# Hybrid decoder block on one core: how many attention turns go with each dense output of the input projection

## The chip, the core and the metric

The kernel runs on one core of a Trainium2 chip. The metric is device time in microseconds of one launch, the median of several runs; a profiled execution of the same program gives the trace. The engines are PE (TensorE, matrix products), DVE (VectorE), ACT (ScalarE), POOL (GpSimd) and SP, which issues most DMAs. Each engine works through its own queue in program order, and waits at an instruction until what that one needs has been signalled by the others.

## The reference

x has 2048 rows of 1024 values.

```python
hn = rmsnorm(h, norm1_g)
proj = hn @ w_in                       # 512 pool columns, then 512 each of q, k, v
y_pool = pool_mixer(u_pool)            # 4 groups of 128, causal means over 2, 4, 8, 16 rows, less the row; then a 128x128 map
o = stick_breaking_attention(q, k, v)  # 8 heads of 64: A[t,s] = sigmoid(z_ts) * prod_(s<j<t) (1 - sigmoid(z_tj))
mixed = concat(rmsnorm(y_pool), rmsnorm(o))
h = h + mixed @ w_out
h = h + relu(rmsnorm(h) @ w_up) ** 2 @ w_down
y = rmsnorm(h)
```

## The kernel before

The rows are cut into four tiles of 512 (tiles 0 to 3). Everything lies transposed: 128 channels on the partitions, 512 rows of a tile along the free axis. Every fp32 product is made of three reduced-precision ones, from a high and a low part of either side; a split (line 145 on ACT for the high part, 146 on DVE for the low) makes these.

The **front** is the first third of the program. It computes the input projection, 16 *dense outputs* per tile: four pool groups (numbers 0 to 3, with windows 2, 4, 8, 16), and q, k and v of four pairs of heads (4 to 15). A dense output is 8 x 3 matmuls of 512 columns (lines 177 to 179) into one of two PSUM buffers `pd`. Its weights are split on ACT and DVE first (`hl<-raw`). Then an evacuation follows: q and k are split and stored to DRAM (`qk`), v is transposed first (`vf`, `ptv`, `vt`). A pool output goes further (`pool_group`): ACT copies it to `u`, DVE adds shifted copies (`s`, line 400; one addition for window 2, up to four for window 16), forms `pl` (line 403), splits it (`pls`, high part on ACT, low part on DVE), and PE maps it with three matmuls (`pp`, lines 410 to 412), which need `pls`.

Between the matmuls of the dense outputs lies the attention, which looks only at the near keys of each row, in 64 *turns* (8 heads x 4 tiles x 2 halves). A turn starts one unit and takes the two before it a stage further. A unit has three stages: logits on PE (`pz`, lines 630 and 631), two sigmoids on ACT (`sh`, `sg`), a mask on POOL (`sg`, line 661), a running product on DVE (`pc`, line 663) and a product (`sg`, line 672); then four transposes on PE (`pta`, line 677) and a split (`at`); then up to six small products on PE (`po`, line 689), and, after every second unit, a sum of halves (`ot`, lines 647 on ACT and 648 on DVE).

How many turns go with a dense output is set by a **ratio**. A dense output adds the ratio to a debt, half of it in its middle and half at its end, and each turn pays back 0.27:

```python
if k == n // 2 - 1:
    advance(state["ratio"] / 2)        # line 181, in products
...
while state["due"] > 0 and todo:       # in advance
    state["due"] -= next(todo[0])      # a turn yields 0.27
```

So a ratio of 0.4 means some three turns with two dense outputs, 0.15 about one with two. When no turn is open, the debt is set to zero. The order of the front is: tile 0 (q, k, v of two pairs, then pool); q, k, v of the other two pairs, for tiles 0 and 1 in turn; tile 1 (pool, then its first two pairs); tile 2 (first two pairs, then pool); the other two pairs for tiles 2 and 3; tile 3 (first two pairs, then pool). Alongside, the next tile is normed piece by piece (`nt`, `h`). What this code emits is a program order with priorities; a scheduler then places each engine's instructions, so that the final order of an engine differs from the order in which the code is written.

Behind the front come the output projection (ratio 0.6, `RATIO_TAIL`, while turns are left) and the feed-forward part, which this code does not touch.

## Time and profile before

| | us |
|---|---|
| median of three runs | 1903.73 (1903.68 to 1907.18) |
| the profiled execution | 1902.05 |
| its span, first to last instruction | 1900.3 |
| PE busy in it | 1868.9 |
| DVE busy in it | 1481.2 |

A PE busy time is the union of its matmuls' spans. A matmul of 512 columns lasts 0.39 us by itself, and the next starts 0.23 us after it where nothing is missing. The granted clock is the share of 2.4 GHz that PE is given; 0.5 is the lower level, 1.2 GHz. The bracket at the end of a timeline row is the idle time of the engine ahead of that instruction, and what ended it.

### The profile page before, as it was taken

Reading aid. Unit: us, or ns where it says so; the run is one execution under the profiler, and the core shown is the slowest. Engines: PE = TensorE matmul, PEld = TensorE weight load, DVE = VectorE, ACT = ScalarE, POOL = GpSimd, SP = SyncE. Lnnn points to the kernel's source line nnn. Section 1 sums busy time; section 2 is a strip of 40 time slices with the busy share of each in tenths; the row PEclk is TensorE's granted clock in tenths of the full one; section 3 lists DMA queues with packets and bytes.
Section 4 is the critical chain, followed back from the end, with each engine's and each line's share of the span. In section 5 each row is a group of like instructions: output and inputs, shape, how many; then the busy total and the mean of one; then the engine's idle time right before and its main releaser. Section 6 shows DMA issues by size and latency. Waiting matters only on the chain.

```text
span 1900.3 us, 26640 instructions
## 1 busy us (share of the span) xinstructions
PE 1868.9 (98%) x8883; PEld 1554.3 (82%) x8883; DVE 1481.2 (78%) x2151; ACT 1025.2 (54%) x1616; POOL 238.5 (13%) x463
## 2 busy tenths in 40 slices
PE   9999999999999999999999999999999999999997
PEld 7788788788888888777888888887888888888886
DVE  6887789678866886778799988786666677988774
ACT  6565567455644465554567555554332665656543
POOL 0233234122321050000000000000010010020120
PEclk9999999999999999999999999999999999999998
DMA  7676596699888777787899888889999899999852
GB/s 226 212 255 201 177 313 224 194 322 315 281 310 312 278 252 254 284 303 274 307 358 328 303 308 281 298 284 333 388 313 330 281 317 307 332 294 341 289 206 91
DMA packets 222164, 535.91 MB, mean 282 GB/s; under 512 B 26048, under 2 KB 32192, under 8 KB 218176
## 3 DMA queue, kind: packets, MB, share of 16 engines
q1 hardware_dynamic: 217264, 525.46, 79.4%
q0 software_dynamic: 4608, 8.39, 2.4%
q8 instruction: 72, 1.18, 0.3%
q14 instruction: 76, 0.62, 0.1%
q10 hardware_dynamic: 144, 0.26, 0.0%
HBM read 349.46 MB, written 184.55 MB: 281 GB/s over the span
## 4 chain that ended last, share of the span: by engine, by line
PE 50%; DMA 5%; DVE 2%; issue 1%; ACT 1%; POOL 0%; SPq 0%; DVEq 0%; ACTq 0%
PE pb L1291 14%; PE pY L1118 13%; PE pb L1468 12%; PE pZ L1118 7%; PE pX L1118 3%; DMA ar<-sd 1%; DMA hn<-hs 1%; DMA ar<-sdi 1%; PE pb L1408 1%; DMA td<-t 0%; DMA t<-in_w_down_dram 0%; DMA b<-in_w_down_dram 0%; DMA wr<-in_w_down_dram 0%; DVE ad L146 0%; DVE hw L146 0%
## 5 line engine op out<-in xcount | busy, mean ns | idle before, releaser
L1118 PE MATMUL pY<-sa,hw 128*128 128x512 f32 x1536 | 366.3, 390 | 1.9 <-ACT u L1041 1.9
L1118 PEld LDWEIGHTS pY<-sa,hw 128*128 128x128 f32 x1536 | 287.9, 188 | 63.0 <-ACT u L1041 3.4
L1291 PE MATMUL pb<-ad,wd 128*128 128x512 f32 x1344 | 305.4, 389 | 0.7 <-DVE ad L146 0.7
L177 PE MATMUL pd<-h,hl 128*128 128x512 f32 x752 | 297.9, 396 | 1.5 <-DVE qk L146 1.3
L178 PE MATMUL pd<-h,hl 128*128 128x512 f32 x752 | 297.0, 395 | 0.3 <-DVE h L146 0.3
L179 PE MATMUL pd<-h,hl 128*128 128x512 f32 x752 | 297.3, 395 | 0.0
L1291 PEld LDWEIGHTS pb<-ad,wd 128*128 128x128 f32 x1344 | 252.1, 188 | 53.8 <-DVE ad L146 1.5
L1468 PE MATMUL pb<-ad,wd 128*128 128x512 f32 x1104 | 253.9, 390 | 0.9 <-ACT ad L145 0.9
L1468 PEld LDWEIGHTS pb<-ad,wd 128*128 128x128 f32 x1104 | 206.5, 188 | 44.6 <-ACT ad L145 1.3
L146 DVE TENSOR_TENSOR ad<-ar,ad 128x1024 fp32r<-128x1024 f32 x160 | 194.1, 1221 | 44.1 <-ACT ad L145 43.5
L145 ACT ACTIVATE ad<-ar 128x1024 fp32r<-128x1024 f32 x160 | 168.4, 1054 | 95.7 <-PE pb L1468 31.9
L1118 PE MATMUL pZ<-sa,hw 128*128 128x512 f32 x768 | 186.8, 390 | 1.7 <-DVE a L1061 1.7
L1118 PEld LDWEIGHTS pZ<-sa,hw 128*128 128x128 f32 x768 | 143.9, 188 | 32.7 <-DVE a L1061 3.0
L145 ACT ACTIVATE hl<-raw 128x512 fp32r<-128x512 f32 x168 | 104.1, 629 | 115.6 <-PE pd L179 76.7
L177 PEld LDWEIGHTS pd<-h,hl 128*128 128x128 f32 x752 | 142.2, 189 | 29.0 <-DVE qk L146 1.8
L179 PEld LDWEIGHTS pd<-h,hl 128*128 128x128 f32 x752 | 142.0, 189 | 28.2 <-DVE hl L146 0.5
L178 PEld LDWEIGHTS pd<-h,hl 128*128 128x128 f32 x752 | 142.2, 189 | 27.1 <-DVE h L146 0.7
L146 DVE TENSOR_TENSOR hl<-raw,hl 128x512 fp32r<-128x512 f32 x168 | 115.1, 690 | 46.9 <-ACT hl L145 46.5
L1035 ACT ACTIVATE a<-a 128x512 f32<-128x512 f32 x96 | 60.1, 629 | 89.6 <-DVE a L1077 38.5
L146 DVE TENSOR_TENSOR hw<-rt,hw 128x512 fp32r<-128x512 f32 x128 | 86.5, 686 | 25.2 <-ACT hw L145 25.1
L145 ACT ACTIVATE wd<-wq 128x1024 fp32r<-128x1024 f32 x56 | 59.4, 1060 | 77.1 <-PE pb L1291 68.4
L146 DVE TENSOR_TENSOR wd<-wq,wd 128x1024 fp32r<-128x1024 f32 x56 | 68.5, 1222 | 34.3 <-ACT wd L145 32.8
(218 smaller groups left out, 2737.3 us busy)
## 6 DMA issues: line engine op xcount, KB each, us to landing
ar<-sd SPq DMA_DIRECT2D x96, 512.0 KB, 5.9
ar<-sdi SPq DMA_DIRECT2D x64, 512.0 KB, 5.6
rb<-in_w_up_dram SPq DMA_DIRECT2D x30, 1024.0 KB, 6.2
sd<-a SPq DMA_DIRECT2D x104, 256.0 KB, 5.2
raw<-in_w_in_dram SPq DMA_DIRECT2D x50, 512.0 KB, 4.6
sdi<-hr SPq DMA_DIRECT2D x96, 256.0 KB, 5.4
wr<-in_w_down_dram SPq DMA_DIRECT2D x48, 512.0 KB, 5.7
sd<-s SPq DMA_DIRECT2D x88, 256.0 KB, 4.9
```

What stands on the lines that cost most here:

```text
L145: nc.scalar.activation(hi, src, AF.Copy)
L146: return nc.vector.tensor_tensor(lo, src, hi.bitcast(F32), ALU.subtract)
L177: nc.tensor.matmul(ps, hl[:, 0, c], hi, start=(k == 0), stop=False)
L178: nc.tensor.matmul(ps, hl[:, 0, c], lo, start=False, stop=False)
L179: last_mm[0] = nc.tensor.matmul(ps, hl[:, 1, c], hi, start=False, stop=(k == n - 1))
L1035: nc.scalar.activation(t, src, AF.Relu)
L1118: nc.tensor.matmul(t, w[:, wx, c], a[:, ax, c % 2], start=first and c == 0 and x == 0, stop=last and c == G - 1 and x == 2, skip_group_che ...
L1291: nc.tensor.matmul(b, t[:, wx, 2 * (kk % 2) + c, i * P:(i + 1) * P], a[:, ax, c], start=p in ("P1", "P5", "P2") and kk == 0 and c == 0 and ...
L1408: nc.tensor.matmul(b[:, cols], block(t, wx, c, n), a[:, ax, c, cols], start=False, stop=(i == 1 and c == 1 and x == 2), skip_group_check=True)
L1468: nc.tensor.matmul(ps[q, n], block(t, wx, c, n), left_[q][:, ax, c], start=(n_ in ("P1", "P3") and kk == 0 and c == 0 and x == 0), stop=(n ...
```

## The change

The table of six ratios becomes a table by tile pair, stretch and kind of output: a pair of numbers stands for (q, k or v; pool), and the middle number is that of the stretch in which two tiles alternate. In the first pair (tiles 0 and 1) the first two stretches keep 0.3 and 0.4; tile 1's own stretch goes from 0.15 to 0.1 for pool and to 0.25 for q, k, v. In the second pair, tile 2's own stretch goes from 0.4 to 0.25 for q, k, v and to 0.1 for pool; tile 3's from 0.3 to 0.4 and to 0.25. The rate is now set at each dense output of these stretches and not once for all of them.

```diff
--- before.py
+++ after.py
@@ -31,7 +31,7 @@
 WINDOWS = (2, 4, 8, 16)
 PAD = 15
 EPS = 1e-6
-RATIO_FRONT = (0.3, 0.4, 0.15, 0.4, 0.4, 0.3)
+PACE = (((0.3, 0.3), 0.4, (0.25, 0.1)), ((0.25, 0.1), 0.4, (0.4, 0.25)))
 RATIO_TAIL = 0.6
 SR = 3
 LB = 4
@@ -510,9 +510,8 @@
 
         a, b = 2 * q, 2 * q + 1
 
-        def rate(i):
-            note(lambda: state.update(ratio=RATIO_FRONT[3 * q + i]))
-        rate(0)
+        def rate(r):
+            note(lambda: state.update(ratio=r))
         if q == 0:
             note(start)
             note(norm1_first)
@@ -520,6 +519,7 @@
         else:
             note(lambda: (load_x(b, bigp), norm1_rms(b), norm1(b), pace(2)))
         for i, c in enumerate((EARLY if q else FIRST) + POOL):
+            rate(PACE[q][0][c in POOL])
             if q == 0 and i == 2:
                 note(lambda: load_x(b, x0p))
             if q == 0 and i == 4:
@@ -532,7 +532,7 @@
             if q and i in (2, 5):
                 attend(a, i // 3)
         note(lambda: (catch_up(len(later)), pool_norm(a)))
-        rate(1)
+        rate(PACE[q][1])
         for h2 in (2, 3):
             note(lambda h2=h2: (norm1_rms(2) if h2 == 2 else None) if q == 0 else attn_norm(0) if h2 == 2 else None)
             for c in range(4 + h2, 16, 4):
@@ -541,8 +541,8 @@
             attend(a, h2)
             attend(b, h2)
         note(lambda: (catch_up(len(later)), (load_acc(0), load_mix(0, KD), attn_norm(1)) if q else norm1(b + 1), pace(1)))
-        rate(2)
         for i, c in enumerate(EARLY + POOL if q else POOL + EARLY):
+            rate(PACE[q][2][c in POOL])
             if q == 0 and i == 4:
                 note(lambda: pool_norm(b))
             if q == 0 and i == 6:
```

What that does to the order of the engines is shown at three places. First DVE at the last pool output of tile 2 (window 16), up to the low part of its split, `pls` of the last row in each piece; before:

```order
L146 TENSOR_TENSOR at_4214<-pta_4209,at_4214 128x512
L400 TENSOR_TENSOR s_4172<-s_4170 128x520
L146 TENSOR_TENSOR hl_4416<-raw_4106,hl_4416 128x512
L663 SCALAR_TENSOR_TENSOR pc_4347<-sh_4352,later_keys_106 128x512
L400 TENSOR_TENSOR s_4174<-s_4172 128x512
L672 TENSOR_TENSOR sg_4354<-sg_4354,pc_4347 128x2x255
L146 TENSOR_TENSOR at_4277<-pta_4272,at_4277 128x512
L403 SCALAR_TENSOR_TENSOR pl_4176<-s_4174,u_4164 128x512
L648 TENSOR_TENSOR ot_4127<-ot_4127,po_4202 64x512
L146 TENSOR_TENSOR at_4343<-pta_4338,at_4343 128x512
L146 TENSOR_TENSOR hl_4419<-raw_4248,hl_4419 128x512
L146 TENSOR_TENSOR pls_4178<-pl_4176,pls_4178 128x512
```

Now:

```order
L663 SCALAR_TENSOR_TENSOR pc_4002<-sh_4007,later_keys_106 128x512
L400 TENSOR_TENSOR s_3965<-s_3963 128x524
L146 TENSOR_TENSOR pls_3908<-pl_3906,pls_3908 128x512
L189 TENSOR_TENSOR ss_4055<-ss_4055,sq_4057 128x512
L672 TENSOR_TENSOR sg_4009<-sg_4009,pc_4002 128x2x255
L400 TENSOR_TENSOR s_3967<-s_3965 128x520
L400 TENSOR_TENSOR s_3969<-s_3967 128x512
L403 SCALAR_TENSOR_TENSOR pl_3971<-s_3969,u_3959 128x512
L648 TENSOR_TENSOR ot_4066<-ot_4066,po_3986 64x512
L663 SCALAR_TENSOR_TENSOR pc_4078<-sh_4083,later_keys_106 128x512
L672 TENSOR_TENSOR sg_4085<-sg_4085,pc_4078 128x2x255
L146 TENSOR_TENSOR pls_3973<-pl_3971,pls_3973 128x512
```

In the first piece three units' `at` splits, a `pc` and an `sg` stand between the additions `s` of line 400 and the pool's `pls`; in the second the last two additions and `pl` follow each other, and rows of two units stand there. From the first `s` of tile 2's first pool output to this `pls` there were 66 rows, and now there are 46.

Second, DVE at the last pool output of tile 1, whose `pl` and `pls` are those numbered 2647 and 2649 in both; before:

```order
L400 TENSOR_TENSOR s_2643<-s_2641 128x520
L146 TENSOR_TENSOR hl_2819<-raw_2695,hl_2819 128x512
L663 SCALAR_TENSOR_TENSOR pc_2777<-sh_2782,later_keys_106 128x512
L648 TENSOR_TENSOR ot_2766<-ot_2766,po_2662 64x512
L400 TENSOR_TENSOR s_2645<-s_2643 128x512
L672 TENSOR_TENSOR sg_2784<-sg_2784,pc_2777 128x2x255
L740 TENSOR_SCALAR zero_2912<-left0_137 128x16
L146 TENSOR_TENSOR at_2773<-pta_2769,at_2773 128x384
L146 TENSOR_TENSOR hl_2822<-raw_2745,hl_2822 128x512
L403 SCALAR_TENSOR_TENSOR pl_2647<-s_2645,u_2635 128x512
L741 TENSOR_REDUCE zall_141<-zero_2912 128x1
L146 TENSOR_TENSOR pls_2649<-pl_2647,pls_2649 128x512
```

Now:

```order
L146 TENSOR_TENSOR hl_2819<-raw_2668,hl_2819 128x512
L668 TENSOR_TENSOR sg_2733<-sg_2733,pc_2726 128x127
L668 TENSOR_TENSOR sg_2733<-sg_2733,pc_2726 128x255
L400 TENSOR_TENSOR s_2645<-s_2643 128x512
L146 TENSOR_TENSOR hl_2822<-raw_2745,hl_2822 128x512
L663 SCALAR_TENSOR_TENSOR pc_2806<-sh_2811,later_keys_106 128x512
L403 SCALAR_TENSOR_TENSOR pl_2647<-s_2645,u_2635 128x512
L648 TENSOR_TENSOR ot_2795<-ot_2795,po_2712 64x512
L672 TENSOR_TENSOR sg_2813<-sg_2813,pc_2806 128x2x255
L146 TENSOR_TENSOR at_2802<-pta_2798,at_2802 128x384
L740 TENSOR_SCALAR zero_2891<-left0_137 128x16
L146 TENSOR_TENSOR pls_2649<-pl_2647,pls_2649 128x512
```

A unit's product of line 663, which stood seven rows ahead of `pl`, stands now in the row just ahead of it, and the rows `ot`, `sg`, `at` and `zero` from ahead of `pl` to between `pl` and `pls`.

Third, PE at the same output, up to the pool's three matmuls; before:

```order
L178 MATMUL pd_2747<-h_1127,hl_2689 128x512
L179 MATMUL pd_2747<-h_1127,hl_2689 128x512
L677 MATMUL pta_2769<-ident_98,sg_2683 128x128 x3
L177 MATMUL pd_2747<-h_1132,hl_2689 128x512
L178 MATMUL pd_2747<-h_1132,hl_2689 128x512
L179 MATMUL pd_2747<-h_1132,hl_2689 128x512
L410 MATMUL pp_2652<-pls_2649,pw_656 128x512
L411 MATMUL pp_2652<-pls_2649,pw_656 128x512
L412 MATMUL pp_2652<-pls_2649,pw_656 128x512
```

Now:

```order
L630 MATMUL pz_2805<-kw_2420,qa_2415 128x256
L631 MATMUL pz_2805<-kw_2420,qb_2416 128x256
L630 MATMUL pz_2805<-kw_2420,qa_2415 128x256
L631 MATMUL pz_2805<-kw_2420,qb_2416 128x256
L689 MATMUL po_2712<-at_2722,vw_2383 64x128
L689 MATMUL po_2712<-at_2722,vw_2383 64x256
L689 MATMUL po_2712<-at_2722,vw_2383 128x128
L689 MATMUL po_2712<-at_2722,vw_2383 64x128
L677 MATMUL pta_2798<-ident_98,sg_2733 128x128 x3
L410 MATMUL pp_2652<-pls_2649,pw_656 128x512
L411 MATMUL pp_2652<-pls_2649,pw_656 128x512
L412 MATMUL pp_2652<-pls_2649,pw_656 128x512
```

The logits `pz` on which that product of line 663 rests stood 29 rows ahead of line 410 before (as `pz` 2776), and stand nine rows ahead of it now (as `pz` 2805).

## Rows read from the trace of the kernel before

**Rows 1.** The page's first part: busy us, share and instructions of each engine.

```profile
PE 1868.9 (98%) x8883; PEld 1554.3 (82%) x8883; DVE 1481.2 (78%) x2151; ACT 1025.2 (54%) x1616; POOL 238.5 (13%) x463
```

**Rows 2.** Busy time by stretch: PE, PEld, DVE, ACT, POOL, granted clock share, DMA.

```profile
206.00:214.00 8.00, 3.79 (x10) 2.53 (x9) 7.30 (x14) 4.67 (x9) 1.96 (x3) 0.80 0.63 192
298.00:332.00 34.00, 34.00 (x196) 29.05 (x194) 33.50 (x51) 23.80 (x45) 17.45 (x19) 1.00 0.68 236
332.00:348.00 16.00, 13.16 (x64) 10.62 (x63) 15.94 (x26) 9.12 (x17) 5.25 (x7) 0.79 0.40 120
348.00:376.00 28.00, 28.00 (x145) 23.75 (x144) 10.22 (x17) 9.16 (x16) 3.48 (x15) 1.00 0.68 201
376.00:400.00 24.00, 24.00 (x143) 20.84 (x142) 18.84 (x26) 14.43 (x29) 9.25 (x24) 1.00 0.94 322
75.00:100.00 25.00, 24.07 (x119) 19.57 (x118) 21.89 (x39) 16.56 (x30) 3.78 (x5) 1.00 0.63 199
100.00:125.00 25.00, 23.81 (x149) 20.43 (x148) 18.90 (x31) 13.21 (x27) 10.69 (x24) 1.00 0.65 192
425.00:450.00 25.00, 24.46 (x139) 20.68 (x138) 21.41 (x32) 15.16 (x29) 4.21 (x8) 1.00 1.02 376
```

**Rows 3.** PE timeline of the tile 1 stretch: start us, us, engine, line.

```profile
205.97 0.40 PE L179 MATMUL pd<-h,hl 128*128 128x512 f32 x1
...
210.35 0.50 PE L410 MATMUL pp<-pls,pw 128*128 128x512 f32 x1 [3.98 <-ACT pls L145]
...
211.07 0.79 PE L411 MATMUL pp<-pls,pw 128*128 128x512 f32 x1 [0.22 <-DVE pls L146]
```

**Rows 4.** DVE timeline of the tile 1 stretch.

```profile
193.65 0.69 DVE L400 TENSOR_TENSOR s<-u 128x526 f32<-128x526 f32 x1
...
205.86 0.65 DVE L648 TENSOR_TENSOR ot<-ot,po 64x512 f32<-64x512 f32 x1
...
207.80 0.17 DVE L740 TENSOR_SCALAR zero<-left 128x16 f32<-128x16 f32 x1
...
207.88 0.55 DVE L146 TENSOR_TENSOR at<-pta,at 128x384 fp32r<-128x384 f32 x1
...
208.95 0.68 DVE L403 SCALAR_TENSOR_TENSOR pl<-s,u 128x512 f32<-128x512 f32 x1
...
210.33 0.69 DVE L146 TENSOR_TENSOR pls<-pl,pls 128x512 fp32r<-128x512 f32 x1 [0.62 <-ACT pls L145]
```

**Rows 5.** ACT and POOL timelines of the tile 1 stretch.

```profile
201.99 0.58 ACT L636 ACTIVATE sh<-pz 128x512 f32<-128x512 f32 x1
...
209.66 0.63 ACT L145 ACTIVATE pls<-pl 128x512 fp32r<-128x512 f32 x1 [2.63 <-DVE pl L403]
...
203.12 3.02 POOL L661 TENSOR_SCALAR_AFFINE_SELECT sg<-sg 128x256 f32<-128x256 f32 x1 [7.92 <-ACT sg L638]
```

**Rows 6.** PE timeline of the tile 2 stretch.

```profile
334.54 0.49 PE L411 MATMUL pp<-pls,pw 128*128 128x512 f32 x1 [0.30 <-DVE pls L146]
...
339.87 0.66 PE L677 MATMUL pta<-ident,sg 128*128 128x128 f32 x4 [1.87 <-DVE at L146]
...
341.19 2.18 PE L689 MATMUL po<-at,vw 128*128 128x256 f32 x12 [0.67 <-DVE ot L648]
```

**Rows 7.** DVE timeline of tile 2's pool outputs, first `s` and last `pls`.

```profile
298.89 0.70 DVE L400 TENSOR_TENSOR s<-u 128x526 f32<-128x526 f32 x1
...
342.37 0.68 DVE L146 TENSOR_TENSOR pls<-pl,pls 128x512 fp32r<-128x512 f32 x1
```

**Rows 8.** DVE groups by shape, 182 to 350 us: count, busy us, mean ns.

```profile
L663 DVE TENSOR_TENSOR_SCAN pc<-sh,later_keys 128x512 f32<-128x512 f32 x21 | 25.6, 1221 | 0.0
...
L672 DVE TENSOR_TENSOR sg<-sg,pc 128x510 f32<-128x510 f32 x22 | 15.3, 697 | 3.6 <-POOL sg L661 3.4
...
L146 DVE TENSOR_TENSOR at<-pta,at 128x512 fp32r<-128x512 f32 x22 | 15.0, 680 | 0.4 <-ACT at L145 0.2
```

**Rows 9.** The tile sg on POOL, all 64: duration ns, least, median, most.

```profile
L661 POOL TENSOR_SCALAR_AFFINE_SELECT sg<-sg x64: 401/674/8157, 92.4 to 534.2; 128x256 f32<-128x256 f32 x64
```

## The prediction

> **What bounds the kernel now.** I read the page's busy times first, then the busy time by stretch, then the timelines of PE, DVE and ACT where PE stands idle, and last the order of the instructions. PE is busy for 1868.9 of 1900.3 us [rows 1], so no order of the same matmuls can win more than the 31 us between. The change adds and removes no instruction; it moves attention turns within the front, so it can only fill or make idle time of PE there. The stretches show that this idle time is nearly all in two places.
>
> The first is at 206 to 214 us, the last pool output of tile 1. PE ends a dense output with the matmul that starts at 205.97, and its next one, the pool's line 410, starts at 210.35 after 3.98 us idle, released by ACT's `pls`; line 411 waits 0.22 more for DVE's [rows 3]. In these 8 us PE is busy for 3.79 and the granted clock is 0.80 [rows 2]. The clock has two levels, 2.4 and 1.2 GHz; a mean of 0.80 over 8 us is 3.2 us at the lower one, and half of that, 1.6 us, is lost. So this place costs 4.2 + 1.6 = 5.8 us.
>
> The second is at 332 to 348 us, the last pool outputs of tile 2. PE waits three times: 0.30 for a `pls`, 1.87 for an `at` split, 0.67 for an `ot` sum, all on DVE [rows 6]. PE is busy for 13.16 of 16 us and the clock is 0.79 [rows 2]: 2.8 us idle, 6.7 us at the lower level and so 3.4 lost, 6.2 us together. What makes PE wait there is the sheer amount of work on DVE: it is busy for 33.5 of 34 us in 298 to 332 and for 15.94 of 16 in the next stretch, while in 348 to 376, just behind, it is busy for 10.22 of 28 [rows 2]. Tile 2's pool work on DVE reaches from its first addition at 298.89 to its last `pls`, which ends at 343.05 [rows 7]: 44.2 us.
>
> **The change, part by part.** How many turns start with each stretch follows from the code alone: a debt of one ratio per dense output, 0.27 paid per turn. Worked through, before and now: tile 0 and the first alternating stretch 16 and 16; tile 1's pool 3 and 2, its q, k, v 3 and 6; tile 2's q, k, v 9 and 5, its pool 6 and 2; the second alternating stretch 11 and 17; tile 3's q, k, v 7 and 9, its pool 5 and 4; the output projection 4 and 3. Both sums are 64. Wherever the code insists that a tile's turns are finished, they are in both orders, so no batch of turns is forced out without matmuls beside it.
>
> *Tile 2.* Four turns leave its four pool outputs and four more leave the six outputs ahead. One unit costs DVE a `pc` (1.22 us), an `sg` (0.70), an `at` (0.68) [rows 8] and half of an `ot` (0.33 [rows 4]): 2.9 us. Now 46 rows stand on DVE where 66 stood, and at the 0.67 us per row of before (44.2 / 66) that is 31 us, 13 less. On PE the new order has 130 matmuls of 512 columns from the end of the first pool output's own to the last pool product, 30 us at the spacing of 0.23, and the small ones of some four units, by their columns 1.2 us each at the same rate: 35 us. So DVE needs 31 us where PE has 35. That is the cover, 4 us of it to spare, and I take all 6.2 us as gone. At worst one wait with its clock loss stays, 3 us of the 6.2.
>
> *The turns that leave* go to 348 to 376 us, where DVE has 17.8 us free and ACT 18.8 [rows 2]. Six more units cost DVE 17.4 us spread over twelve dense outputs, some 70 us. The same pace of 0.4 with the same mix stands in the first alternating stretch, where PE lost 0.93 us in 75 to 100 and 1.19 in 100 to 125 [rows 2]: small waits, no clock loss. So the new stretch costs between 0 and 2 us; I take 0.5, since DVE has no norm of a next tile to make beside it as it had there.
>
> *Tile 1.* Here the counts say one turn less with the pool outputs, but the order says something else. The last pool output's line 410 stands as far behind its dense matmuls as before, and 25 rows of DVE work between its first `s` (193.65 us) and its `pl` (208.95) [rows 4] become 21, which at 0.61 us each takes 2.4 us off. What is new is that the row just ahead of `pl` is the product `pc` of a unit whose logits stand just ahead of line 410 on PE. DVE cannot pass it. From the end of these logits: ACT's `sh` 0.58 [rows 5], `pc` 1.22 [rows 8], `pl` 0.68 [rows 4], ACT's `pls` 0.63 [rows 5], in sum 3.1 us; PE has some 0.7 us of small matmuls and transposes in the meantime. So line 410 waits 2.4 us in place of 4.0. But `pls` on DVE, for which line 411 waits, now has `ot` 0.65, `zero` 0.17, `at` 0.55 [rows 4] and `sg` 0.70 [rows 8] between it and `pl`: from the logits' end 0.58 + 1.22 + 0.68 + 2.07 + 0.69 = 5.2 us, less 0.7 for PE's work: line 411 starts 4.5 us behind the dense output's end, and before it did so at 211.07 - 206.2 = 4.9. The two waits together stay as long, 4 to 5 us, and the clock loss with them. What queues behind them is the same, PE's next dense output and on DVE two `qk` splits. So I take 0 for tile 1, between a win of 3 (the clock never falls) and a loss of 3 (a second stretch as slow).
>
> In that chain `sg` needs POOL's mask first. POOL took 3.02 us for one at this place [rows 5], and 0.40 to 8.16 us elsewhere [rows 9], for the same shape. With 3.0 us in place of the median 0.67 the `sg`, and with it line 411, comes about 1 us later than above. The Trainium skill, SBUF — State Buffer, "Who interferes with whom", has a rule for it: a DVE instruction with two SBUF inputs and a GpSimd instruction that reads SBUF contend, and the later of the two waits until the other has finished. The spread of the mask's times on a busy DVE agrees with that; by this rule the mask is long here again, since `pc`, `pl` and `ot`, each with two SBUF inputs, run one behind the other.
>
> *Tile 3 and the rest* get 9 turns in place of 7 and 4 in place of 5. Of the stretches of 25 us that lie there, the one where PE lost most lost 0.54 [rows 2]. Two units more add 5.8 us of DVE work over six dense outputs, 33 us: 0 to 1 us, taken as 0.
>
> The sum: -6.2 + 0.5 + 0 = -5.7 us against the profiled execution's 1902.05, so 1896.35. The median of the runs is 1.7 above that execution, so I expect 1898.0.
>
> **The rivals.**
>
> A: tile 1 gets better too. The `pc` ahead of `pl` comes in time or the clock stays up: 3 us more off, 1895. For it speaks that line 410 waits less; against it that line 411 does not.
>
> B: the waits come back elsewhere. Six more units between the alternating outputs, or the mask at tile 1 at its long times with a second stretch at the low clock, return 2 to 5 us of the 6.2: 1900 to 1903.5, not to be told from no change. For it speaks the spread of the mask's times [rows 9]; against it the free time of DVE behind tile 2 [rows 2]. By the rule of the Trainium skill alone it would be the 1 us named above, 1899.
>
> C: the change doesn't do what it says. If the wait at tile 2 comes from the pool outputs' own chain (additions, `pl`, two splits) and not from the turns among them, it stays: 1903.5. Against it: the 1.87 us wait is on an `at`, the 0.67 on an `ot`, both attention's own [rows 6].
>
> D: slower. With fewer turns between them the dense outputs follow each other faster, and PE reaches a pool product sooner: between the matmuls of tile 2's third pool output and its line 410 stood 61 dense matmuls, and now stand 48, 3 us less. If DVE is not ahead by as much, PE waits at each of the four products for some 1.5 us, with the clock low after each as at tile 1: 4 x (1.5 + 1.6) = 12.4 us in place of 6.2, so 6 us slower: 1910. It decides where DVE is more than the 4 us to spare behind PE at the first `s`. Against it stand the 31 us of DVE work in 35 us.
>
> **How the numbers follow.** The forecast (1896.5 to 1899.5) gets 0.58, A 0.08, B 0.18, C 0.06, D 0.10. The range from 1894.5 to 1904 holds the forecast, most of A, and B and C; D is left out. A measurement of this kernel can tell 0.2%, 3.8 us, from no change. Faster than 1899.9 are the forecast but for a twentieth, A and a quarter of B: 0.68. Within 3.8 us are most of B, C and a little of the forecast and of D: 0.23. Slower is most of D: 0.09.
>
> **What would show it.** In the changed profile the stretch of tile 2's pool outputs has no wait above 0.5 us on PE and a granted clock of 1.00, DVE is busy for less than 0.95 of it, and the alternating outputs behind it have DVE at 0.7 or more in place of 10.22 of 28. At tile 1's last pool output line 410 waits 2 to 3 us and line 411 another 1.5 to 2.5, with a granted clock of about 0.8 once more. The forecast is wrong if line 410 or 411 waits in tile 2, if a clock below 0.9 appears behind 240 us, or if tile 1 shows no wait.

## The result, and the profile after

The changed kernel takes 1911.69 us (median of 16 runs, 1906.86 to 1916.06), the kernel before 1903.17 (16 runs, the three given above among them): a ratio of 1.0045, with a 95% interval of 1.0036 to 1.0055. So it is 8.5 us slower, where 5.7 us faster was predicted, and the result lies outside the range. The profiled execution took 1912.45 us.

The page's first part, which answers to [rows 1]:

```profile
PE 1873.2 (98%) x8883; PEld 1557.1 (81%) x8883; DVE 1482.9 (78%) x2151; ACT 1024.8 (54%) x1616; POOL 226.5 (12%) x463
```

Its PE row is 4.3 us higher though the matmuls are the same: more of them ran at the lower clock (the granted clock over the whole execution is 0.992, and 0.995 before). Busy time by stretch, the columns as in [rows 2] (PE, PEld, DVE, ACT, POOL, granted clock, DMA); the first five stretches answer to it, the last two are new:

```profile
206.00:214.00 8.00, 3.50 (x10) 2.35 (x10) 8.00 (x15) 5.21 (x11) 2.85 (x3) 0.80 0.91 279
298.00:332.00 34.00, 34.00 (x175) 28.62 (x174) 32.54 (x50) 21.92 (x41) 15.08 (x13) 1.00 0.62 203
332.00:348.00 16.00, 16.00 (x98) 13.77 (x97) 13.40 (x22) 9.66 (x19) 2.97 (x11) 1.00 0.83 237
348.00:376.00 28.00, 28.00 (x170) 24.34 (x169) 22.29 (x32) 17.82 (x33) 8.26 (x21) 1.00 0.84 280
376.00:400.00 24.00, 24.00 (x142) 20.69 (x142) 19.80 (x29) 13.81 (x26) 8.47 (x25) 1.00 0.82 247
250.00:265.00 15.00, 9.90 (x47) 8.08 (x46) 10.82 (x17) 8.25 (x16) 1.72 (x2) 0.90 0.85 307
710.00:722.00 12.00, 8.79 (x30) 6.94 (x30) 2.66 (x4) 2.54 (x6) 3.32 (x8) 0.72 0.07 29
```

The two new stretches in the kernel before:

```profile
250.00:265.00 15.00, 14.24 (x80) 12.01 (x79) 14.76 (x23) 11.75 (x23) 3.74 (x6) 1.00 0.97 324
710.00:722.00 12.00, 12.00 (x59) 10.10 (x58) 7.75 (x14) 5.81 (x12) 1.05 (x6) 1.00 0.34 98
```

Tile 2's place is mended: PE is busy for all of 332 to 348 us at a clock of 1.00, in place of 13.16 of 16 at 0.79, and none of the three waits of [rows 6] is left. But at 250 to 265 and at 710 to 722, where next to nothing was missing before, PE now stands idle for 5.1 and 3.2 us, and the clock falls to 0.90 and 0.72.

To add this up I use one measure for all kernels, the **loss**: by how much each PE matmul starts later than its predecessor at full clock allows (0.227 us after one of 512 columns, 0.119 after 256, 0.06 after 128, 0.112 after a transpose), summed over a stretch, a start sooner than that counted off. It holds idle time and what a lower clock costs together. Over the whole program it is 45.3 us before and 55.9 after; span less loss is 1855.0 and 1854.8, so the loss holds the whole difference of the two executions. By place, with a second execution of the changed kernel from another session:

| loss in us | before | after | after, again |
|---|---|---|---|
| 200-220: tile 1's last pool output | 6.4 | 8.3 | 8.2 |
| 250-270: from tile 1 to tile 2 | 1.3 | 8.3 | 8.8 |
| 330-350: tile 2's last pool outputs | 6.9 | 0.4 | 0.4 |
| 350-550: second alternating stretch, tile 3 | 3.8 | 7.0 | 6.1 |
| 690-720: start of the feed-forward | 0.1 | 6.3 | 4.7 |
| all the rest | 26.8 | 25.6 | 24.4 |

**Tile 1's last pool output**, first the timeline of PE; these two answer to [rows 3, 4]:

```profile
209.86 0.49 PE L410 MATMUL pp<-pls,pw 128*128 128x512 f32 x1 [3.30 <-ACT pls L145]
211.55 0.79 PE L411 MATMUL pp<-pls,pw 128*128 128x512 f32 x1 [1.19 <-DVE pls L146]
```

And on DVE:

```profile
207.19 1.22 DVE L663 TENSOR_TENSOR_SCAN pc<-sh,later_keys 128x512 f32<-128x512 f32 x1
208.32 0.83 DVE L403 SCALAR_TENSOR_TENSOR pl<-s,u 128x512 f32<-128x512 f32 x1
209.07 0.67 DVE L648 TENSOR_TENSOR ot<-ot,po 64x512 f32<-64x512 f32 x1
209.67 0.68 DVE L672 TENSOR_TENSOR sg<-sg,pc 128x510 f32<-128x510 f32 x1
210.28 0.54 DVE L146 TENSOR_TENSOR at<-pta,at 128x384 fp32r<-128x384 f32 x1
...
210.82 0.67 DVE L146 TENSOR_TENSOR pls<-pl,pls 128x512 fp32r<-128x512 f32 x1
```

The `pc` of line 663 stands ahead of `pl` (line 403) and `ot`, `sg`, `at` between `pl` and `pls`, as the order said. Line 410 waits 3.30 us in place of 3.98, line 411 1.19 in place of 0.22.

**From tile 1 to tile 2**, in the timelines of the kernel before, PE first (a row's bracket: idle before it, and the releaser):

```profile
243.60 0.60 PE L454 MATMUL ptv<-ident,vf 128*128 128x128 f32 x4
...
256.07 0.50 PE L177 MATMUL pd<-h,hl 128*128 128x512 f32 x1 [0.76 <-DVE qk L146]
```

And on ACT:

```profile
244.29 0.59 ACT L145 ACTIVATE vt<-ptv 128x512 fp32r<-128x512 f32 x1
244.77 1.15 ACT L145 ACTIVATE mix<-nt 128x512 fp32r<-128x512 f32 x2
...
251.33 0.63 ACT L145 ACTIVATE mix<-nt 128x512 fp32r<-128x512 f32 x1 [2.25 <-DMA vs<-vt]
...
254.69 0.60 ACT L145 ACTIVATE qk<-pd 128x512 fp32r<-128x512 f32 x1
```

The same in the changed kernel, PE first:

```profile
247.90 0.60 PE L454 MATMUL ptv<-ident,vf 128*128 128x128 f32 x4
...
262.79 0.79 PE L177 MATMUL pd<-h,hl 128*128 128x512 f32 x1 [5.10 <-DVE qk L146]
```

And on ACT:

```profile
248.53 0.60 ACT L145 ACTIVATE vt<-ptv 128x512 fp32r<-128x512 f32 x1 [0.26 <-DMA vw<-vs]
249.03 1.15 ACT L145 ACTIVATE mix<-nt 128x512 fp32r<-128x512 f32 x2
...
257.71 0.63 ACT L145 ACTIVATE mix<-nt 128x512 fp32r<-128x512 f32 x1 [2.35 <-DMA vs<-vt]
...
260.71 0.61 ACT L145 ACTIVATE qk<-pd 128x512 fp32r<-128x512 f32 x1
```

PE needs a PSUM buffer that DVE's and ACT's `qk` of tile 2's first q output set free. `qk` stands on ACT behind the last `mix`, a split of tile 1's pool norm; and `mix` waits until the store of `vt` to DRAM (`vs`) has landed, because `mix`, `qk`, `pls` and `vt` take turns in a ring of three SBUF buffers. That wait was there before, too. From the transposes of the last v (line 454) to the release of PE it took 12.5 us before (243.60 to 256.07) and 14.9 now (247.90 to 262.79). In the meantime PE had work for 11.7 us (until 255.31) and has now for 9.8 (until 257.69): logits of three units (line 630) lay in it before and of one lie in it now. So of the 4.3 us by which PE's wait grew, 2.4 are a longer chain and 1.9 are missing work. In the chain the store is late: SP issued it 2.3 us after DVE's part of `vt` was ready (252.62, ready at 250.34), where it had done so at once before (245.75, ready at 245.72). The second of its two halves landed at 257.62, and `mix` started at 257.71.

**Start of the feed-forward**, in the timelines of the changed kernel. Line 231 spreads the inverse roots `yrlast` of the last tile's rows, eight matmuls for each half; POOL computes them step by step, here from 705.05 on. PE:

```profile
708.93 1.00 PE L231 MATMUL pr<-identr,yrlast 128*128 128x128 f32 x8
...
713.65 1.61 PE L231 MATMUL pr<-identr,yrlast 128*128 128x128 f32 x6 [3.21 <-POOL yrlast L834]
```

And on POOL:

```profile
705.05 0.56 POOL L214 TENSOR_SCALAR v<-v 128x4 int32<-128x4 int32 x1 [21.65 <-DVE v L213]
...
706.90 1.06 POOL L224 TENSOR_TENSOR v<-v 128x4 f32<-128x4 f32 x1
...
713.67 0.20 POOL L835 TENSOR_TENSOR yrlast<-v,yrlast 128x4 fp32r<-128x4 f32 x1
```

The second spread waits 3.21 us for POOL. In the kernel before it stood 80 PE instructions behind the first and not 10, and ran at 721.00, long after POOL had ended at 711.44; PE there:

```profile
703.78 1.00 PE L231 MATMUL pr<-identr,yrlast 128*128 128x128 f32 x8
...
721.00 1.00 PE L231 MATMUL pr<-identr,yrlast 128*128 128x128 f32 x8
```

And on POOL:

```profile
700.25 6.98 POOL L214 TENSOR_SCALAR v<-v 128x4 int32<-128x4 int32 x1 [14.59 <-DVE v L213]
...
711.24 0.20 POOL L835 TENSOR_TENSOR yrlast<-v,yrlast 128x4 fp32r<-128x4 f32 x1
```

### The profile page after: what moved, and what is told of

Its sections match the earlier page's. It is cut to its first block, busy times and chain, and to the rows that moved or that the text cites. A ratio compares the mean times of both kernels' runs of the same rounds, so it can differ in the third digit from the quotient of the medians.

```text
span 1910.7 us, 26646 instructions
## 1 busy us (share of the span) xinstructions
PE 1873.2 (98%) x8883; PEld 1557.1 (81%) x8883; DVE 1482.9 (78%) x2151; ACT 1024.8 (54%) x1616; POOL 226.5 (12%) x463
## 4 chain that ended last, share of the span: by engine, by line
PE 64%; DVE 14%; DMA 14%; issue 4%; ACT 2%; POOL 2%; SPq 1%; DVEq 0%; ACTq 0%; POOLq 0%
PE pb L1291 14%; PE pb L1468 12%; PE pY L1118 9%; PE pd L177 6%; PE pd L178 5%; PE pd L179 5%; PE pZ L1118 4%; PE pX L1118 2%; DMA t<-in_w_down_dram 2%; DVE hw L146 2%; DMA hn<-hs 2%; DMA ar<-sd 1%; DMA td<-t 1%; DVE hl L146 1%; PE po L689 1%
## 5 line engine op out<-in xcount | busy, mean ns | idle before, releaser
L146 DVE TENSOR_TENSOR hw<-rt,hw 128x512 fp32r<-128x512 f32 x128 | 86.3, 686 | 26.8 <-ACT hw L145 26.6
```

The source lines that it names most:

```text
L146: return nc.vector.tensor_tensor(lo, src, hi.bitcast(F32), ALU.subtract)
```

## The experiments

**Parts of the change.** Each row of the table alone, the others as before:

```diff
 before, in the same form:  (((.3, .3), .4, (.15, .15)), ((.4, .4), .4, (.3, .3)))
+tile 1 alone:              (((.3, .3), .4, (.25, .1)),  ((.4, .4), .4, (.3, .3)))
+tile 2 alone:              (((.3, .3), .4, (.15, .15)), ((.25, .1), .4, (.3, .3)))
+tile 3 alone:              (((.3, .3), .4, (.15, .15)), ((.4, .4), .4, (.4, .25)))
```

> Only tile 1's own stretch has the new ratios (0.25 for q, k, v and 0.1 for pool); the second pair keeps 0.4, 0.4, 0.3 as before. My theory: the changed kernel's loss is four separate waits, each from its own place: (a) +2 us at tile 1's last pool output, from the product of line 663 that stands right ahead of pl there; (b) +7 us at 250 to 262 us, from the fewer turns with tile 2's first q, k, v, which let PE come to the next PSUM buffer sooner than its qk evacuation; (c) +6 us at 715 us, from the second spread of the last norm, which the scheduler has put right behind the first; (d) +3 us in tile 3. By it this kernel has (a) alone: tile 2's waits stay as before (6 to 8 us at 330 to 350), nothing above 1.5 us at 250 to 262, nothing at 715: 1 to 4 us slower than before, ratio 1.001 to 1.002. Rival for (b): the wait at 250 comes from the more frequent turns with tile 1's q, k, v, whose loads and splits delay the store of vt; then it stands here too, 6 to 8 us there, and the kernel is 8 to 11 us slower, ratio about 1.005.

> Only tile 2's own stretch has the new ratios (0.25 for q, k, v and 0.1 for pool); tile 1 keeps 0.15, tile 3 keeps 0.3. My theory (fewer turns with tile 2's first q, k, v uncover the qk evacuation): the wait of 5 us at 250 to 262 us with its clock loss is here, 6 to 8 us, the 6 to 7 us at 330 to 350 are gone, tile 1's pool wait is as before (4 us idle), no wait at 715: within 2 us of before, ratio 0.999 to 1.001. Rival (the wait at 250 is tile 1's doing): no wait above 1.5 us there, so 5 to 7 us faster than before, ratio 0.9965.

> Only tile 3's own stretch has the new ratios (0.4 for q, k, v and 0.25 for pool); the rest as before. My theory: the small waits at 470 to 520 us and the one at 565 us come from these, 2 to 4 us, and the places at 206, 255 and 340 us are as before: 2 to 4 us slower, ratio 1.001 to 1.002. Rival: they come from the turns deferred out of tile 2 into the alternating outputs, and this kernel is the same as before, ratio 1.000.

Tile 1 alone: 1.0045 (1.0027 to 1.0062), 1911.41 us; its profiled execution took 1904.05 and so stands for the others only in part. In it PE waits 2.87 us at 250 to 270 (loss 3.6), where before's loss was 1.3. Tile 2 alone: 1.0015 (1.0003 to 1.0027); 330 to 350 loses 0.3 and 250 to 270 no more than before, but a new wait has come at 550 to 570, in the output projection, with a loss of 8.1. Tile 3 alone: 1.0014 (1.0001 to 1.0028); it mends nothing at tile 2 (5.7) and loses 6.8 at 350 to 550, 3.0 more than before. So the wait at 250 to 270 goes with tile 1's numbers, and the gain at 330 to 350 with tile 2's. The theory of the first two expectations, that tile 2's fewer turns make the wait, failed; the rival that they name, tile 1's turns, fits, though with a loss of 3.6 us and not 6 to 8. The wait of the run with tile 1 alone, on PE:

```profile
246.69 0.60 PE L454 MATMUL ptv<-ident,vf 128*128 128x128 f32 x4
...
260.94 0.50 PE L177 MATMUL pd<-h,hl 128*128 128x512 f32 x1 [2.87 <-DVE qk L146]
```

The chain from the transposes to PE's release takes 14.3 us here, 1.8 more than before, while PE has work for 11.4, only 0.3 less.

**Two smaller cuts**: the change without its tile 1, and tile 2's pool outputs alone.

```diff
+tile 1 undone:             (((.3, .3), .4, (.15, .15)), ((.25, .1), .4, (.4, .25)))
+tile 2's pool alone:       (((.3, .3), .4, (.15, .15)), ((.4, .1), .4, (.3, .3)))
```

> The change with tile 1's ratio of before (0.15 for all); tiles 2 and 3 as changed. Theory T (the wait at 250 to 262 us needs tile 1's new pace, as the run with tile 1 alone had 2.9 us of it and the run with tile 2 alone none; and the early second spread of the feed-forward is an accident of this one order): no wait above 1.5 us at 250 to 270, the spreads 80 PE instructions apart and no wait of POOL's yrlast at 700 to 720, tile 2's stretch without loss: 1897 to 1901. Rival U (fewer turns in tile 2's first outputs suffice): the loss of 8 us at 250 to 270 stays, about 1906. Rival V (other orders bring losses of their own, as the output projection did at 550 to 570 in the run with tile 2's numbers): a new place with 3 us or more, 1902 to 1906.

> Only the ratio of tile 2's pool outputs is changed (0.4 to 0.1); tile 2's q, k, v stay at 0.4, tiles 1 and 3 as before. Theory P (the pool outputs' turns alone made the wait at 332 to 348 us, and the rest of the change only costs): the loss of 6.9 us there falls below 1.5, the places at 250 to 270 and 700 to 720 stay as before (1.3 and below 0.5), and the time is 3 to 6 us below before's, unless the output projection at 550 to 570 loses its 8 us as in the run with tile 2's own numbers. Rival Q (the turns with tile 2's q, k, v are as much to blame): 3 us or more of the loss stay at 332 to 348, and the time is within 2 us of before's.

> The run with tile 2's pool outputs alone at 0.1, again: if its gain is the order's and not one execution's, the ratio to before is 0.993 to 0.998 once more, and 330 to 350 us loses below 1 us.

Without tile 1's numbers the change is faster than before: 1900.04 us, 0.9978 (0.9961 to 0.9996). The feed-forward's spreads stand 80 PE instructions apart again in this order. The loss at 250 to 270 is 0.8, at 690 to 720 0.1, at 330 to 350 0.3. Tile 2's pool ratio alone does better still: 1898.22 us, 0.9954 (0.9935 to 0.9974), and again 1897.11, 0.9968 (0.9958 to 0.9978). So the turns among tile 2's four pool outputs made the wait there, and the ones with its q, k and v need not leave. The row of tile 2's place in the first of these:

```profile
332.00:348.00 16.00, 16.00 (x98) 13.89 (x97) 12.11 (x18) 7.45 (x15) 7.21 (x21) 1.00 0.67 202
```

**The changed kernel again**, to see whether its losses belong to the order:

> The changed kernel again, unchanged, to see which of its losses come back in another execution. If they belong to its order, the waits at 250 to 270 (8.2 us lost) and 700 to 720 (6.3) return within 1 us, and tile 1's at 200 to 220 (8.3) within 2; a loss that belongs to one execution is gone or halved. Time 1911 within 2.

1911.15 us, 1.0033 (1.0022 to 1.0045); the table above has its losses. All come back, that at 690 to 720 with 4.7 us in place of 6.3.

**The wait between tiles 1 and 2.** Four runs with the changed table. First a fourth buffer in the ring, then pieces of the norm issued sooner, so that two of the four `mix` stand ahead of `vt`:

```diff
-tag="st", ..., bufs=3)          # mix, pls, qk, vt
+tag="st", ..., bufs=4)          # first run
...
-if q == 0 and i == 6:                            # second run
-    note(lambda: pace(2))
+if q == 0 and i == 4:
+    note(lambda: pace(3))
```

> The changed kernel with four buffers instead of three in the ring that mix, pls, qk and vt share on SBUF; nothing else in the code differs, but the scheduler's order differs from row 387 of PE on, and its spreads of the feed-forward stand 80 PE instructions apart again. Theory R (the wait at 250 to 262 us, 5.1 us of PE behind DVE's qk, comes from the ring: mix cannot be written before the store of vt that used the same buffer has ended): ACT's mix does not wait for that store, PE's wait there falls below 1.5 us, the loss of 8.2 us in 250 to 270 falls to 1 to 3, the wait of 3.2 us at 715 is gone, and the time is 11 to 13 us below the changed kernel: 1898 to 1901. Rival S (PE simply reaches the next dense output too soon, whatever the ring, since no turn stands between): the wait stays at 3 us or more, only the 6 us at 715 come back: about 1905. Tile 1's wait at 200 to 220 stays at 6 to 8 us by both.

> The changed kernel with one difference: the pieces of tile 1's pool norm are issued three per dense output from its first q, k, v output on, in place of one or two and, later, two. On ACT two of the four mix splits then stand ahead of vf and vt and two behind; the table of ratios is the changed one, and the feed-forward's spreads stand 10 PE instructions apart as there. Theory M (the 5 to 6 us wait at 250 to 262 us is a queue: qk stands on ACT and DVE behind a mix that waits until the store of vt has freed its buffer of the ring): with two mixes gone from behind vt, ACT's mix does not wait for vs<-vt, PE's wait there falls below 2 us and the loss in 250 to 270 from 8.2 to below 3; the wait at 715 stays; 1904 to 1906. Rival S (qk itself waits for the store, or PE simply comes too early by the turns that are missing there): the wait stays at 3.5 us or more, 1909 to 1911.

Both failed: 1.0049 (1.003 to 1.0068) and 1.004 (1.0025 to 1.0054). With four buffers it is the last `mix` that meets the store of `vt`; with the pieces ahead it is `qk` itself. The timeline of the first, on ACT:

```profile
256.16 0.63 ACT L145 ACTIVATE mix<-nt 128x512 fp32r<-128x512 f32 x1 [3.47 <-DMA vs<-vt]
```

And on PE:

```profile
259.88 0.79 PE L177 MATMUL pd<-h,hl 128*128 128x512 f32 x1 [4.23 <-DVE qk L146]
```

That of the second, on ACT:

```profile
261.88 0.60 ACT L145 ACTIVATE qk<-pd 128x512 fp32r<-128x512 f32 x1 [2.52 <-DMA vs<-vt]
```

And on PE:

```profile
263.26 0.79 PE L177 MATMUL pd<-h,hl 128*128 128x512 f32 x1 [3.67 <-DVE qk L146]
```

So moving the wait to the next in the ring is not enough. Then `vt` got a buffer of its own, and in another run its stores were issued by POOL and not by SP, where a load stands ahead of them:

```diff
-vt = pa.tile(..., tag="st", name="vt", bufs=3)
+vt = pa.tile(..., tag="vt", name="vt", bufs=1)            # third run
...
-nc.sync.dma_start(vs[2 * c + e][j]..., vt...)
+nc.gpsimd.dma_start(vs[2 * c + e][j]..., vt...)           # fourth run
```

> The changed kernel with a buffer of its own for vt (one), so that mix, pls and qk share the ring of three among themselves and nothing behind vt waits for its store; the scheduler then puts the four mix splits ahead of vt on ACT, and the feed-forward's spreads stand 80 PE instructions apart again. Theory S2 (whatever takes vt's buffer next, a mix in the changed kernel or a qk in the run with the early pieces, waits for the store of vt, which SP issues late behind loads that wait; that wait is what PE meets at 250 to 264 us): neither mix nor qk waits for vs<-vt, the loss at 250 to 270 falls below 2.5 us, 700 to 720 loses below 1, and the time is 1897 to 1900. Rival U2 (the stores are incidental: with the table of the change PE simply comes to q of tile 2 before DVE and ACT can): 4 us or more of loss stay there, 1902 to 1905.

> The changed kernel with the stores of vt (line 458) issued by POOL in place of SP; rings and table as changed, and ACT's order around 250 us as in the changed kernel. The spreads of the feed-forward stand 32 PE instructions apart (10 in the changed kernel, 80 before), so 1 to 6 us may stay at 700 to 720. If the store is late because SP stands at a load ahead of it (2.1 us at raw in the changed kernel), vs<-vt is issued within 1 us of DVE's vt, and ACT's mix and PE's wait at 250 to 262 come 2 to 2.5 us sooner: the loss there falls from 8.2 to 3 to 5.5. If the queue doesn't matter and the store's own 4 to 6 us from issue to landing do, the loss stays at 7 or more.

With a buffer of its own the wait is gone: the loss at 250 to 270 is 0.2, the lowest of all kernels, and no `mix` or `qk` waits for `vs<-vt`. That fits the ring as the way by which the store holds PE, as the rows of `mix` and `qk` above have it; by itself it doesn't prove it, since the scheduler also moved `vt` behind the last `mix`, and no row of `mix` was left between `vt` and `qk`. Yet this kernel took 1908.85 us, 1.0026 (1.0011 to 1.0042), since the output projection now loses 10.4 us at 550 to 570, as it did with four buffers (9.9) and with tile 2 alone. PE there:

```profile
558.36 1.86 PE L205 MATMUL pm<-inv,ss 128*128 128x1 f32 x8 [7.94 <-DVE ss L189]
```

Line 205 sums squares that ACT can form only when `ol` has been loaded. SP issued these loads at 548.47, behind a load of weights at 548.04; in the run with tile 2's pool alone, repeated, they were issued at 539.74, and nothing was lost. That isn't all of it: with tile 2 alone they were issued at 541.91, and PE still waited 5.1 us at line 205. What decides it I didn't try.

With the stores on POOL's queue nothing is won: 1.0072 (1.0055 to 1.0089), a loss of 8.0 at 250 to 270. The timeline of POOL:

```profile
251.95 1.13 POOL L458 DMA_DIRECT2D vs<-vt  x2 [2.36 <-DVE vt L146]
```

And on ACT:

```profile
259.38 0.63 ACT L145 ACTIVATE mix<-nt 128x512 fp32r<-128x512 f32 x1 [3.75 <-DMA mx<-mix]
```

The stores were issued 0.6 us after `vt` was ready (251.38) and not 2.3, and the `mix` was not written sooner for that: it started 7.4 us after the first of these issues. But the stores took longer, 6.3 and 7.3 us from issue to landing in place of 4.4 and 4.6, and the trace names the store of an earlier `mix`, 7.3 us from issue to landing, as the last releaser here. So the run put one delay in the place of another, and doesn't tell what SP's late issue costs. That a late issue isn't needed is shown by the last run below: there the store was issued 0.1 us after `vt` was ready, and the wait is there all the same. The view of the DMA issues of the changed kernel (count, KB each, and at the end the median us from issue to landing):

```profile
vs<-vt SPq DMA_DIRECT2D x32, 256.0 KB, 4.3
```

**The feed-forward's spread**, first alone and then together with the earlier pieces:

```diff
-nc.tensor.matmul(t, w[:, wx, c], ...
+mm = nc.tensor.matmul(t, w[:, wx, c], ...
...
-spread(pr, yrlast[:, i])
+with tc.issue_after(mm.ins):
+    spread(pr, yrlast[:, i])
```

> The changed kernel, with the two spreads of the last norm's roots held behind the matmuls that they follow in the code, so that PE does not come to the second one before POOL has made its root. The order of PE up to there is that of the changed kernel. My theory: the wait of 3.2 us and the clock loss behind it at 715 us go, and nothing else moves: 5 to 7 us faster than the changed kernel, about 1905.5, ratio to before 1.0005 to 1.002. Rival: PE's wait there is made by POOL and DVE being late as a whole, and comes back at the next consumer (the stretch up to 760 us): no gain, ratio 1.004 to 1.005.

> The run before with the feed-forward's second spread held behind the last matmul of its own half of the sums, as in the run with the late spread: both suspected losses of the changed kernel are taken out, and the table of ratios stays the changed one. If the two are all that stands between the prediction and the result, the losses at 250 to 270 and 700 to 720 are below 3 and 2 us, the rest of the front as in the changed kernel, and the time 1897 to 1900.5, within 2 us of the prediction's 1898. If something else is missing, 1903 or more with a loss at another place.

With the spread held back the changed kernel takes 1905.18 us, 1.0012 (0.9997 to 1.0028). Line 231 waits no longer:

```profile
719.86 1.00 PE L231 MATMUL pr<-identr,yrlast 128*128 128x128 f32 x8
...
723.94 1.00 PE L231 MATMUL pr<-identr,yrlast 128*128 128x128 f32 x8
```

That is some 6 us of the 8.5, with a loss of 2.1 left at 690 to 720; 250 to 270 keeps its 8.2. The run meant to mend both came to 1903.93, 1.0008 (0.9997 to 1.0018). It was no test of the sum, as the pieces didn't mend the wait between the tiles (loss 5.8): of what it set out to show, only the part on the spread stands.

**Tile 1's own wait.** No turns with its pool outputs, tile 2's pool at 0.1; the first with the spread held back, the second without:

```diff
+first:                      (((.3, .3), .4, (.15, 0)),   ((.4, .1), .4, (.3, .3)))
+second:                     (((.3, .3), .4, (.2, 0)),    ((.4, .1), .4, (.3, .3)))
```

> Tile 2's pool outputs at 0.1 and all else as before, as in the run with that number alone, and tile 1's pool outputs at 0 in place of 0.15; the second spread is held back as in the run with the late spread. Is tile 1's own wait at its last pool output (6 us of loss at 200 to 220 in every kernel so far) made by the turns among these outputs? If yes, the loss there falls to 3 or less and the time to 1894 to 1896. If no (the chain of additions, pl and splits behind the dense output is what is late, whatever the turns), 5 us or more stay and the time is 1898 within 2; or the turns that leave bring a new wait of 3 us or more at tile 1's q, k, v, 1899 to 1903.

> The run without turns at tile 1's pool outputs, but with nothing held back in the feed-forward (its spreads stand 80 PE instructions apart by themselves in this order) and 0.2 in place of 0.15 for tile 1's q, k, v; tile 2's pool outputs at 0.1, all else as before. If the turns among tile 1's pool outputs set most of its wait, the loss at 200 to 220 is 2 to 4 us in place of 6 to 7, that at 690 to 720 below 1, and the time 1894 to 1897, the best so far. If the gain there comes back as a wait in tile 1's q, k, v or at 250 to 270, 2 us or more of loss appear at 220 to 270 and the time is 1897 to 1900.

1899.60, 0.9984 (0.9971 to 0.9996), and 1904.43, 0.9997 (0.9983 to 1.0011). The waits of lines 410 and 411 in the first:

```profile
205.30 0.50 PE L410 MATMUL pp<-pls,pw 128*128 128x512 f32 x1 [1.20 <-ACT pls L145]
206.83 0.50 PE L411 MATMUL pp<-pls,pw 128*128 128x512 f32 x1 [1.03 <-DVE pls L146]
```

They are 2.2 us together and not 4.2, and the loss at 200 to 220 is 3.2, the lowest measured. In the second the two are 1.34 and 1.53 us, and the loss is 5.3, with a granted clock of 0.79 in 206 to 214 there and of 1.00 in the first. So the turns among the pool outputs make a third to a half of that wait. The first isn't better than tile 2's pool ratio alone, since 3.9 us are lost at 690 to 720. In the second, with 0.2 for q, k and v, the wait at 250 to 270 is back with a loss of 7.1, on PE:

```profile
241.29 0.60 PE L454 MATMUL ptv<-ident,vf 128*128 128x128 f32 x4
...
258.37 0.79 PE L177 MATMUL pd<-h,hl 128*128 128x512 f32 x1 [4.82 <-DVE qk L146]
```

The two runs differ in more than one number, so what the one lost against the other isn't settled, but the place fits all others: in the seven profiled executions with 0.15 for tile 1's q, k, v (before, tile 2 alone, tile 3 alone, tile 1 undone, tile 2's pool alone twice, the first run here) 250 to 270 lost 0.8 to 2.6 us (the 2.6, in the first run here, are for the most part another wait, of 1.6 us on DVE's `sg`). In the ten with 0.2 or 0.25 it lost 3.6 to 8.8, but for the one in which `vt` had its own buffer.

What differs there can be read from the traces. All times are in us from the transposes of tile 1's last v (line 454) on; PE's wait is its release less the end of its work:

| | store of `vt` issued | landed | PE released | PE's work ends | PE's wait |
|---|---|---|---|---|---|
| before | 2.2 | 7.7 | 12.5 | 11.7 | 0.8 |
| tile 2 alone | 2.2 | 7.4 | 11.4 | 10.7 | 0.7 |
| tile 1 undone | 2.2 | 7.0 | 11.0 | 10.7 | 0.3 |
| tile 1 alone | 3.6 | 8.9 | 14.3 | 11.4 | 2.9 |
| after | 4.7 | 9.7 | 14.9 | 9.8 | 5.1 |
| after, again | 3.1 | 10.8 | 16.0 | 9.8 | 6.2 |
| 0.2 and no pool turns | 4.0 | 11.2 | 17.1 | 12.3 | 4.8 |

The store lands 6.4 to 8.6 us after the transposes in the seven executions with 0.15, and 8.9 to 12.6 in the ten with more. With tile 2 alone PE has less work than before and waits no longer, since the chain is shorter too; in the last row it has more work than before and waits 4.8 us. So the wait follows the later landing, and the work that PE has meanwhile sets how much of it shows.

## Why the prediction was wrong

**Tile 2, -6.2 us: right.** Its loss fell from 6.9 to 0.4, DVE is busy for 13.40 of 16 us, the clock is 1.00. DVE's work from the first `s` (302.35) to the end of the last `pls` (333.43) took 31.1 us, and 31 was worked out. What was wrong is the share: four fewer turns with the pool outputs do all of it.

**The deferred turns, +0.5: right in its place.** In 348 to 376 us DVE went from 10.22 to 22.29 of 28, and PE is busy for all of it.

**Tile 1's last pool output, 0: right in kind.** Lines 410 and 411 wait 4.49 us together; 4 to 5 was said, and 4.20 it was before. The split was not as said: 3.30 for line 410 (2 to 3) and 1.19 for line 411 (1.5 to 2.5), so that the sum came out by luck. The clock of 206 to 214 is 0.80 as before, but in the 4 us behind it is 0.54 in place of 0.97, and the loss rose by 1.9. That rise isn't steady: the run with the spread held back has the same PE order up to there and lost 6.8, against 6.4 before.

**The step that failed first: tile 1's q, k and v had no term.** The prediction counted 3 turns there before and 6 now, and then spoke only of the last pool output; "What queues behind them is the same" was taken to cover the rest, and tile 1 got 0. What the runs showed in its place is a wait at 250 to 270 us, 7.0 us more of loss than before, that comes with tile 1's numbers. With more turns at tile 1's q, k, v the store of the last `vt` lands later, and `mix` and `qk` stand behind it: PE's release came 14.9 us after the transposes in place of 12.5. At the same time PE's work there shrank from 11.7 us to 9.8. A smaller cover without the longer chain does no harm, as tile 2 alone shows (work of 10.7, a chain of 11.4, a wait of 0.7); the longer chain does with nearly all of the cover left (tile 1 alone: 11.4, 14.3, 2.9). What makes the store late stays open: SP issues it later, just behind a turn's loads and a load of weights, and it took up to 7.3 us to land, and no run parted the two. Rows of before showed the warning: PE waited 0.76 us at just that point, and ACT's `mix` 2.25 for `vs<-vt`. The cover was used up already. The loss is 0.8 when tile 1's numbers are undone, and 0.2 when `vt` leaves the ring; no run took it away with all else equal, so its price in time is known as loss alone.

**The step that failed second: "so it can only fill or make idle time of PE there",** that is, in the front. The scheduler places all instructions of the program in one go, and with another order of the front a spread of the feed-forward moved by 70 PE instructions. That cost 6.2 us in loss and, measured in its own run, 6 us of time. The orders of the two kernels hold the move; the prediction has no term for that part, whose code is unchanged. The sum by measured terms: -6.5 (tile 2), +1.9 (tile 1), +7.0 (between the tiles), +6.2 (spread), +3.2 (350 to 550) and -1.2 (all the rest) make 10.6, against 10.4 between the two spans. The prediction's 31 us as the most that any order could win is too little for a like reason: PE's busy time holds the matmuls that ran at the lower clock, and the loss of the kernel before, idle time and clock together, is 45.3 us.

**Tile 3 and the rest, 0 to 1: too small in this order.** 350 to 550 lost 3.2 and 2.3 us more than before. Tile 3's numbers alone make 3.0, but with tile 1 undone the same numbers make none (3.7). What decides that stays open.

**The rivals.** D had the sign, but its place, tile 2's pool products, has no wait at all now. B had the kind, waits that come back elsewhere, but looked at the alternating outputs and the mask and allowed 2 to 5 us. POOL's mask at tile 1 was named with a rule of the Trainium skill (SBUF — State Buffer, "Who interferes with whom"); it took 1.73 us here, twice the median of 0.86, and DVE's `sg` didn't wait for it, so the rule changed nothing. (The prediction counts `ot` among the instructions with two SBUF inputs, but its input `po` lies in PSUM.) Of what would show the forecast wrong, "a clock below 0.9 behind 240 us" came true at 710 us.

## What to carry to other kernels

When work is moved, ask of every place what it was covering there and what it will now stand in front of. A wait of some tenths of a us behind a long chain marks a cover that is just used up: it grows by all that is taken from the cover and by all that makes the chain longer, here 1.9 and 2.4 us. Where a scheduler places the whole program, compare the orders to the end, also where the source is the same, and price every instruction that waits for another engine and moves forward. And try the parts of a change one by one: here one number of the six that changed was worth more than all of them.

## What the runs showed of the hardware

The same POOL instructions of 4 columns took from 0.19 to 1.06 us, and line 214 took 6.98 us in the kernel before and 0.56 in the changed one (rows above). The long one ran from 700.25 to 707.23, while DVE worked without a gap until 707.18:

```profile
705.90 1.28 DVE L146 TENSOR_TENSOR hw<-rt,hw 128x512 fp32r<-128x512 f32 x2
708.68 0.69 DVE L1061 TENSOR_TENSOR a<-pZ,u 128x512 f32<-128x512 f32 x1 [1.51 <-ACT u L1041]
```

The Trainium skill (SBUF — State Buffer, "Who interferes with whom") has DVE instructions with two SBUF inputs and GpSimd instructions that read SBUF block one another, the later until the earlier is done. The rows agree in kind, but the POOL instruction waited through nine DVE instructions and not one; all nine have two SBUF inputs. In the changed kernel line 214 ended at 705.61, just behind a DVE instruction of that kind (`hw`, until 705.56), and the next on DVE (`a`, line 1047) has one of its inputs in PSUM. No run here tried it alone, and the profile's times on POOL are rough.

The two halves of the store of `vt` looked at here, 256 KB each, took 3.8 to 7.3 us from issue to landing in the seventeen executions, and an engine that wanted the buffer next waited for it: ACT's `mix` 2.35 us in the changed kernel.
